# A rotary-embedding kernel bound by its transfers: tables on every fourth partition, and a store issued only when the loads in front of it are nearly done

## The chip, the cores and the metric

The kernel runs on one core of one Trainium2 chip. The metric is the device time of one execution in microseconds (us). The profile's span, first instruction to last, is 1.7 to 2.2 us shorter than the time; what lies between is not in the trace. All runs quoted here are of the fast state, with a granted clock of 1.0.

## The reference, cut to what matters

```python
batch, seq, heads, dim = (16, 512, 16, 64)
x1, x2 = x[..., :32], x[..., 32:]
a, b = x1[..., :16], x1[..., 16:]          # cos, sin: [512, 32], of which the first 16 columns are used
first  = a * cos[..., :16] - b * sin[..., :16]
second = a * sin[..., :16] + b * cos[..., :16]
out = concatenate([first, second, x2])     # x2 passes through
```

`x` has 33.55 MB. It is read once and written once.

## The kernel before

It cuts `x` into T = 4 tiles of 8.39 MB (128 partitions x 64 KB: K = 16 sequence positions of 4 KB each) and turns them in place in a ring of three tile buffers. All loads and stores of `x` go through one queue, that of SyncE (SP), in the order of the program (67.11 MB in the page's q1; store 0, issued at 44.14 us, has its first packet at 51.71, when the first engine has ended the loads in front). The two tables go through the software queue of GpSimd (POOL; 0.13 MB in q0). PB = 32 rows of a table hold 16 positions each; REP = 4 copies of them fill 128 partitions.

```python
stage = const_pool.tile([PB, 2, K, HF], fp32)
table = const_pool.tile([P, 2, K, 2, Q], fp32)
# ...
nc.gpsimd.dma_start(out=stage[:, 0].rearrange("p k j -> p (k j)"), in_=cosf)
nc.gpsimd.dma_start(out=stage[:, 1].rearrange("p k j -> p (k j)"), in_=sinf)
load(0, 0, K0)              # K0 = 4: the first quarter of tile 0
load(0, K0, K)
load(1)
load(2, 0, KC)              # KC = 8: half of tile 2
for r in range(REP):
    nc.vector.tensor_copy(out=table[r * PB : (r + 1) * PB]..., in_=stage...)   # cut
# rotate(t, lo, hi): four VectorE instructions on rows lo..hi of tile t (mul, mul, sub, add)
rotate(0, 0, K0)
rotate(0, K0, (K0 + K) // 2)
rotate(0, (K0 + K) // 2, K)
store(0)
load(2, KC, K)              # stands behind store 0
load(3)                     # takes tile 0's buffer: waits until store 0 has landed
for t in range(1, T):
    rotate(t, 0, KC)
    rotate(t, KC, K)
    store(t)
```

The transfers therefore change direction three times: loads to store 0 at about 52 us, store 0 to loads at about 71 us, loads to store 1 at about 100 us. These three places are called the joints below.

Of the kernel before, what the change touches and what calls it, by code (L numbers as in the profile page):

```python
# [1 line left out]

# [4 lines left out]


@with_exitstack
def kernel(  # L10
    ctx: ExitStack,
    tc: tile.TileContext,
    x: bass.AP,
    cos: bass.AP,
    sin: bass.AP,
    out: bass.AP,
):
    nc = tc.nc
    fp32 = mybir.dt.float32
    P = 128  # L20
    B, S, H, D = x.shape
    Q = D // 4
    HF = D // 2



    K = 16
    T = B * S // (P * K)
    PB = S // K
    REP = P // PB  # L30
    R = H * D
    NS = 3
    KC = K // 2
    K0 = K // 4

    xf = x.rearrange("b s h d -> (b s h d)").rearrange("(t p f) -> t p f", t=T, p=P)
    of = out.rearrange("b s h d -> (b s h d)").rearrange("(t p f) -> t p f", t=T, p=P)
    cosf = cos.rearrange("(p k) j -> p (k j)", k=K)
    sinf = sin.rearrange("(p k) j -> p (k j)", k=K)

    const_pool = ctx.enter_context(tc.tile_pool(name="const", bufs=1))
    b_pool = ctx.enter_context(tc.tile_pool(name="bp", bufs=1, space=bass.MemoryType.PSUM))


    ring = const_pool.tile([P, NS, K, H, D], fp32)
    stage = const_pool.tile([PB, 2, K, HF], fp32)
    table = const_pool.tile([P, 2, K, 2, Q], fp32)

    def rows(t, lo, hi):
        return ring[:, t % NS, lo:hi].rearrange("p k h d -> p (k h d)")  # L50

    def load(t, lo=0, hi=K):
        nc.sync.dma_start(out=rows(t, lo, hi), in_=xf[t, :, lo * R : hi * R])  # L53

    def store(t, lo=0, hi=K):
        nc.sync.dma_start(out=of[t, :, lo * R : hi * R], in_=rows(t, lo, hi))

    nc.gpsimd.dma_start(out=stage[:, 0].rearrange("p k j -> p (k j)"), in_=cosf)  # L58
    nc.gpsimd.dma_start(out=stage[:, 1].rearrange("p k j -> p (k j)"), in_=sinf)  # L59
    load(0, 0, K0)  # L60
    load(0, K0, K)
    load(1)
    load(2, 0, KC)


    for r in range(REP):
        nc.vector.tensor_copy(  # L67
            out=table[r * PB : (r + 1) * PB].rearrange("p t k c j -> p (t k) c j"),
            in_=stage.rearrange("p t k j -> p (t k) j")[:, :, 0:Q]
            .unsqueeze(2)  # L70
            .to_broadcast((PB, 2 * K, 2, Q)),
        )
    C = table[:, 0].rearrange("p k c j -> p k (c j)")
    Sn = table[:, 1].rearrange("p k c j -> p k (c j)")

    def rotate(t, lo, hi):
        n = hi - lo
        x1 = ring[:, t % NS, lo:hi, :, 0:HF]
        c = C[:, lo:hi].unsqueeze(2).to_broadcast((P, n, H, HF))
        s = Sn[:, lo:hi].unsqueeze(2).to_broadcast((P, n, H, HF))  # L80
        b_full = b_pool.tile([P, KC, H, HF], fp32, name="b_t")
        b_t = b_full[:, 0:n]
        nc.vector.tensor_mul(out=b_t, in0=x1, in1=s)  # L83
        nc.vector.tensor_mul(out=x1, in0=x1, in1=c)  # L84
        nc.vector.tensor_sub(  # L85
            out=x1[:, :, :, 0:Q], in0=x1[:, :, :, 0:Q], in1=b_t[:, :, :, Q:HF]
        )
        nc.vector.tensor_add(  # L88
            out=x1[:, :, :, Q:HF], in0=x1[:, :, :, Q:HF], in1=b_t[:, :, :, 0:Q]
        )  # L90

    rotate(0, 0, K0)
    rotate(0, K0, (K0 + K) // 2)
    rotate(0, (K0 + K) // 2, K)
    store(0)
    load(2, KC, K)
    load(3)
    for t in range(1, T):
        rotate(t, 0, KC)
        rotate(t, KC, K)  # L100
        store(t)


# [1 line left out]
_INS = ['x', 'cos', 'sin']  # L105
_OUTS = [((16, 512, 16, 64), 'float32')]


# [23 lines left out]
```

## Time and profile before

| | |
|---|---|
| time, median of 6 runs | 161.91 us (161.74 to 162.52) |
| span of the profiled run | 160.1 us |
| DMA engines busy | 97.8% of the span by the SP queue |
| VectorE busy | 110.0 us, 69% |
| 64 KB packet on one engine, usual | 2.418 us |

The page and the chain are shown and read in the prediction below. One more view is needed for what follows: the rate between joints. A window's rate counts each packet where it starts, and the 16 engines start their 64 KB packets in bunches about 2.4 us apart, so I put the edges of the windows between bunches. Each then holds whole packets. Columns: window, its length, VectorE busy (instructions), GpSimd busy (instructions), granted clock, DMA share, GB/s. The kernel before, for the first half of tile 2, for the rest of tile 2 and most of tile 3, and for the last 16 load packets ahead of store 1:

```profile
41.95:51.70 9.75, 9.68 (x4) 0.00 (x0) 1.00 1.01 430
...
80.70:97.50 16.80, 16.70 (x6) 0.00 (x0) 1.00 1.01 437
97.50:100.05 2.55, 0.40 (x1) 0.00 (x0) 1.00 0.97 411
```

Almost nothing is lost ahead of store 0 (430 GB/s; 0.10 us by the packet records). The last window holds 16 packets of 64 KB in 2.55 us, edges included; at 2.418 us each they could not do better than that by more than 0.13 us.

In the text and tables below, "loss" is worked out from the packet records: the summed durations of the packets of a stretch, less their bytes at 2.418 us for 64 KB, divided by 16 engines. A packet that the edge of the stretch cuts counts by the share of its time that lies inside, and the 4-byte writes that close a transfer (192 in the kernel before, 16 after each of 12 transfers) are left out. Idle time of an engine is no part of this loss and is given apart. Each loss is that of one profiled execution. "The loss from 4 us to tile 0's landing" is the measure of what the tables cost. In kernels that load tile 0 whole, about 0.2 us of it is the slow first 64 KB packet, which runs on past 4 us: counted over the packets that start after 4 us alone, it is 0.73 us in the kernel before.

### The profile page before, as it was taken

The numbers are of one execution on the slowest core, as the hardware profiler recorded it, in microseconds if no ns is written. First come the engines' busy times: TensorE is split into PE (matmuls) and PEld (weight loads), VectorE is DVE, ScalarE is ACT, GpSimd is POOL, SyncE is SP. The second block draws the span as 40 slices with busy tenths as digits, with TensorE's granted clock in tenths as the row PEclk, the third lists the DMA queues.
The fourth block names the chain that finished last, engine by engine and source line by source line (L and its number), as shares of the span: only waits on it lengthen the run. The fifth ranks groups of instructions, "written<-read, shape, count | busy, mean of one in ns | idle before, by whom it ended". The sixth has DMA issues, their size and how long they took to land.

```text
span 160.1 us, 109 instructions
## 1 busy us (share of the span) xinstructions
DVE 110.0 (69%) x40; POOL 1.3 (1%) x6
## 2 busy tenths in 40 slices
DVE  0069709999999999999999994799999900000000
POOL 3000000000000000000000000000000000000000
DMA  6999999699699799899996996996996996996991
GB/s 197 385 504 454 393 459 524 262 524 491 295 401 581 328 524 409 377 393 418 483 540 295 491 524 262 524 524 262 524 524 262 524 524 262 524 491 295 524 459 66
DMA packets 1504, 67.24 MB, mean 420 GB/s; under 512 B 192, under 2 KB 192, under 8 KB 224
## 3 DMA queue, kind: packets, MB, share of 16 engines
q1 hardware_dynamic: 1440, 67.11, 97.8%
q0 software_dynamic: 64, 0.13, 0.2%
HBM read 33.69 MB, written 33.55 MB: 420 GB/s over the span
## 4 chain that ended last, share of the span: by engine, by line
DMA 50%; DVE 28%; DVEq 1%; issue 0%; SPq 0%
DMA ring<-in_x_dram 32%; DMA out_dram<-ring 18%; DVE b_t L83 10%; DVE ring L84 10%; DVE ring L85 5%; DVE ring L88 3%; DVEq L127 1%; SPq L53 0%; DVEq L83 0%
## 5 line engine op out<-in xcount | busy, mean ns | idle before, releaser
L83 DVE TENSOR_TENSOR b_t<-ring,table 128x4096 f32<-128x4096 f32 (+2 forms) x9 | 35.6, 3959 | 8.2 <-DMA ring<-in_x_dram 8.0
L84 DVE TENSOR_TENSOR ring<-ring,table 128x4096 f32<-128x4096 f32 (+2 forms) x9 | 35.6, 3950 | 0.3
L85 DVE TENSOR_TENSOR ring<-ring,b_t 128x2048 f32<-128x2048 f32 (+2 forms) x9 | 18.4, 2049 | 0.3
L88 DVE TENSOR_TENSOR ring<-ring,b_t 128x2048 f32<-128x2048 f32 (+2 forms) x9 | 18.4, 2042 | 0.0
L67 DVE COPY table<-stage 32x1024 f32<-32x1024 f32 x4 | 2.7, 684 | 9.2 <-DMA stage<-in_sin_dram 9.1
L58 POOL DMA_DIRECT2D stage<-in_cos_dram x1 | 0.6, 631 | 0.8 <-PEq L127 0.8
L59 POOL DMA_DIRECT2D stage<-in_sin_dram x1 | 0.5, 498 | 0.0
L116 POOL MEMSET const-bfloat16-1.0<- 128x1 bf16 x1 | 0.1, 102 | 0.0
L116 POOL MEMSET const-float32-0.0<- 128x1 f32 x1 | 0.1, 99 | 0.2 <-issue 0.2
L116 POOL MEMSET const-float32-1.0<- 128x1 f32 x1 | 0.1, 99 | 0.0
L116 POOL MEMSET const-uint8-127<- 128x1 uint8 x1 | 0.1, 99 | 0.0
## 6 DMA issues: line engine op xcount, KB each, us to landing
ring<-in_x_dram SPq DMA_DIRECT2D x2, 4096.0 KB, 43.9
ring<-in_x_dram SPq DMA_DIRECT2D x1, 6144.0 KB, 22.4
ring<-in_x_dram SPq DMA_DIRECT2D x1, 2048.0 KB, 8.5
stage<-in_cos_dram POOLq DMA_DIRECT2D x1, 64.0 KB, 6.0
stage<-in_sin_dram POOLq DMA_DIRECT2D x1, 64.0 KB, 7.2
out_dram<-ring SPq DMA_DIRECT2D x4, 36.4
ring<-in_x_dram SPq DMA_DIRECT2D x2, 35.0
```

The source lines that it names most:

```text
L58: nc.gpsimd.dma_start(out=stage[:, 0].rearrange("p k j -> p (k j)"), in_=cosf)
L59: nc.gpsimd.dma_start(out=stage[:, 1].rearrange("p k j -> p (k j)"), in_=sinf)
L67: nc.vector.tensor_copy(out=table[r * PB : (r + 1) * PB].rearrange("p t k c j -> p (t k) c j"), in_=stage.rearrange("p t k j -> p (t k) j" ...
L83: nc.vector.tensor_mul(out=b_t, in0=x1, in1=s)
L84: nc.vector.tensor_mul(out=x1, in0=x1, in1=c)
L85: nc.vector.tensor_sub(out=x1[:, :, :, 0:Q], in0=x1[:, :, :, 0:Q], in1=b_t[:, :, :, Q:HF])
L88: nc.vector.tensor_add(out=x1[:, :, :, Q:HF], in0=x1[:, :, :, Q:HF], in1=b_t[:, :, :, 0:Q])
L116: nc = _bacc.Bacc("TRN2", target_bir_lowering=False, num_devices=1)
L127: with _tile.TileContext(nc) as tc:
```

## The change

Its intent has two parts. The tables are to be written on partitions 0, 4, ..., 124 in place of 0 to 31, and VectorE then shuffles them together. And a store is not to stand in the queue long before its turn: tile 0 is turned whole, so that store 0 is issued at about 50 us, and store 1 waits until 14/16 of tile 3 has landed.

```diff
-    K0 = K // 4
+    KL = 14
-    stage = const_pool.tile([PB, 2, K, HF], fp32)
+    stage = const_pool.tile([P, 2, K, HF], fp32)
+    spun = const_pool.tile([P, 2 * K, Q], fp32)
+    packed = const_pool.tile([PB, 2 * K, Q], fp32)
-    nc.gpsimd.dma_start(out=stage[:, 0]..., in_=cosf)      # cut; sin likewise
-    load(0, 0, K0)
-    load(0, K0, K)
+    nc.vector.memset(stage[:, :, :, 0:Q], 0.0)
+    spread = stage.rearrange("(j b) t k i -> j b t (k i)", b=REP)
+    nc.gpsimd.dma_start(out=spread[:, 0, 0], in_=cosf)
+    nc.gpsimd.dma_start(out=spread[:, 0, 1], in_=sinf)
+    load(0)
+    PQ = PB // REP
+    nc.vector.stream_shuffle(out=spun[:], in_=stage..., mask=[j % PQ * REP for j in range(PB)])
+    for q in reversed(range(REP)):
+        n = PQ * (q + 1)
+        nc.vector.tensor_copy(out=packed[0:n], in_=spun[q * PB : q * PB + n])
     # the four table copies now read packed
-    rotate(0, 0, K0)
-    rotate(0, K0, (K0 + K) // 2)
-    rotate(0, (K0 + K) // 2, K)
-    store(0)
+    turn(0)                       # rotate both halves, then store
     load(2, KC, K)
-    load(3)
-    for t in range(1, T): ...
+    near = load(3, 0, KL)
+    load(3, KL, K)
+    tc.add_manual_dep(turn(1).ins, near.ins.name, ...)     # store 1 waits for near
+    turn(2)
+    turn(3)
```

More of the change, by code (lines that the diff above doesn't have):

```diff
@@ L52, in load @@
     def load(t, lo=0, hi=K):
-        nc.sync.dma_start(out=rows(t, lo, hi), in_=xf[t, :, lo * R : hi * R])
+        return nc.sync.dma_start(out=rows(t, lo, hi), in_=xf[t, :, lo * R : hi * R])
     def store(t, lo=0, hi=K):
-        nc.sync.dma_start(out=of[t, :, lo * R : hi * R], in_=rows(t, lo, hi))
-    nc.gpsimd.dma_start(out=stage[:, 0].rearrange("p k j -> p (k j)"), in_=cosf)
-    nc.gpsimd.dma_start(out=stage[:, 1].rearrange("p k j -> p (k j)"), in_=sinf)
-    load(0, 0, K0)
-    load(0, K0, K)
+        return nc.sync.dma_start(out=of[t, :, lo * R : hi * R], in_=rows(t, lo, hi))
+    nc.vector.memset(stage[:, :, :, 0:Q], 0.0)
[3 more added lines that the diff above has]
+    load(0)
     load(1)
     load(2, 0, KC)
+    PQ = PB // REP
+    nc.vector.stream_shuffle(
+        out=spun[:],
+        in_=stage.rearrange("p t k j -> p (t k) j")[:, :, 0:Q],
+        mask=[j % PQ * REP for j in range(PB)],
+    )
+    for q in reversed(range(REP)):
+        n = PQ * (q + 1)
+        nc.vector.tensor_copy(out=packed[0:n], in_=spun[q * PB : q * PB + n])
     for r in range(REP):
@@ L68 @@
             out=table[r * PB : (r + 1) * PB].rearrange("p t k c j -> p (t k) c j"),
-            in_=stage.rearrange("p t k j -> p (t k) j")[:, :, 0:Q]
-            .unsqueeze(2)
-            .to_broadcast((PB, 2 * K, 2, Q)),
+            in_=packed.unsqueeze(2).to_broadcast((PB, 2 * K, 2, Q)),
         )
@@ L76, in rotate @@
     def rotate(t, lo, hi):
-        n = hi - lo
         x1 = ring[:, t % NS, lo:hi, :, 0:HF]
-        c = C[:, lo:hi].unsqueeze(2).to_broadcast((P, n, H, HF))
-        s = Sn[:, lo:hi].unsqueeze(2).to_broadcast((P, n, H, HF))
+        c = C[:, lo:hi].unsqueeze(2).to_broadcast((P, hi - lo, H, HF))
+        s = Sn[:, lo:hi].unsqueeze(2).to_broadcast((P, hi - lo, H, HF))
         b_full = b_pool.tile([P, KC, H, HF], fp32, name="b_t")
-        b_t = b_full[:, 0:n]
+        b_t = b_full[:, 0 : hi - lo]
         nc.vector.tensor_mul(out=b_t, in0=x1, in1=s)
@@ L90, in rotate, with turn @@
         )
-    rotate(0, 0, K0)
-    rotate(0, K0, (K0 + K) // 2)
-    rotate(0, (K0 + K) // 2, K)
-    store(0)
-    load(2, KC, K)
-    load(3)
-    for t in range(1, T):
+    def turn(t):
         rotate(t, 0, KC)
         rotate(t, KC, K)
-        store(t)
+        return store(t)
+    turn(0)
+    load(2, KC, K)
+    near = load(3, 0, KL)
+    load(3, KL, K)
+    tc.add_manual_dep(
+        turn(1).ins,
+        near.ins.name,
+        mybir.DependencyInfo(mybir.DependencyClass.Sync, mybir.DependencyReason.DATA),
+        reason="the store follows the loads at the DMA engines",
+    )
+    turn(2)
+    turn(3)
 _INS = ['x', 'cos', 'sin']
```

## The prediction

> **What bounds the kernel now.** I read the page's DMA rows first, then its chain of waits, then the order of instructions in time, and last the records of single DMA packets that the trace keeps. The page says that the 16 DMA engines are the whole story:
>
> ```profile
> span 160.1 us, 109 instructions
> ...
> DVE 110.0 (69%) x40; POOL 1.3 (1%) x6
> ...
> DMA  6999999699699799899996996996996996996991
> ...
> q1 hardware_dynamic: 1440, 67.11, 97.8%
> q0 software_dynamic: 64, 0.13, 0.2%
> ```
>
> VectorE (DVE) is busy 110.0 of 160.1 us, the DMA engines 97.8% of the span. The dips to 6 in the DMA row are not idle time: packets are up to 64 KB long and are booked where they start. I checked that in the packet records: between 3 us and 158 us the 16 engines' packets cover the time without a gap that I can find (the summed durations differ from 16 times the elapsed time by under 0.3 us).
>
> The chain of waits names both engines, but this is how it was followed back and not proof that DVE costs anything:
>
> ```profile
> DMA 50%; DVE 28%; DVEq 1%; issue 0%; SPq 0%
> DMA ring<-in_x_dram 32%; DMA out_dram<-ring 18%; DVE b_t L83 10%; DVE ring L84 10%; DVE ring L85 5%; DVE ring L88 3%; DVEq L127 1%; SPq L53 0%; DVEq L83 0%
> ```
>
> The DVE stretches in it (the first tile's 20 us and the last tile's 27 us) lie beside transfers that were already queued. The order in time shows it for the first store:
>
> ```profile
> 0.74 1.88 SPq L53 DMA_DIRECT2D ring<-in_x_dram  x4
> ...
> 9.13 2.77 DVE L67 COPY table<-stage 32x1024 f32<-32x1024 f32 x4 [9.13 <-DMA stage<-in_sin_dram]
> ...
> 23.66 3.37 DVE L83 TENSOR_TENSOR b_t<-ring,table 128x3072 f32<-128x3072 f32 x1 [4.71 <-DMA ring<-in_x_dram]
> ...
> 44.14 0.35 SPq L56 DMA_DIRECT2D out_dram<-ring  x1
> 44.53 28.14 SPq L53 DMA_DIRECT2D ring<-in_x_dram  x2
> 72.77 0.38 SPq L56 DMA_DIRECT2D out_dram<-ring  x1
> ```
>
> Store 0 is issued at 44.14 us, while the packet records have the loads in front of it running until 51.7 to 52.2 us (each engine ends at its own time). So it waits 8 us in the queue and hides the issue cost. The second store, issued at 72.77 us, stands behind the rest of tile 2 and tile 3, which end at 100.1 to 100.6 us.
>
> The budget, from the packet records: a 64 KB packet takes 2.418 us, so 16 engines move 16 x 65536 / 2.418 us = 433.7 GB/s, and the page's 67.24 MB need 155.0 us. The first packet starts at 1.75 us, the last ends at 158.60, the span ends at 160.1. That is 1.75 head + 156.85 transfers + 1.5 tail. Only 156.85 - 155.0 = 1.8 us of the transfers is loss, and this is where it lies, each as the mean over 16 engines:
> - about 0.6 us in the first packet of each engine (1.21 us on average where 16 KB take 0.604 at the full rate), and about 0.1 us of staggered starts;
> - about 0.65 us from 5.0 to 8.6 us, where the two table transfers pass: the 48 packets of 16 KB that start after 5.3 us take 0.777 us on average and not 0.611;
> - about 0.4 us scattered over everything after 23 us, most of it in the 32 KB packets (1.213 to 1.217 us where half of 2.418 is 1.209) and the seams; the rest is engines that end up to 0.54 us before the last.
>
> [...]The trace before has the tables on 0 to 31 and the slow packets just there[...].
>
> **The change, part by part.**
> *Tables on every fourth partition.* Same bytes (0.13 MB). Of the 0.65 us lost around them, I expect half or a little more to go, since the two table transfers also insert themselves between packets (that part stays): -0.35 us, with 0 to -0.65 possible. This is ahead of everything in the queue, so it shifts the end one for one.
> *The extra DVE work.* A memset of 128x512, which the table transfers now wait for[...], four copies of 32x512 (half of the measured 684 ns each, 1.4 us), and the four table copies as before (2.7 us). The tables arrive later too: [...]packets of 64 KB to queue behind (2.4 us each, one for each table, where it was 0.6). Landing at 12 to 13 us and not 9.1, plus 4.7 us, gives tables at 17 to 18 us. Tile 0 lands at about 23 us. Cost on the path: 0, with some 5 us to spare.
> *Tile 0 loaded and turned whole.* Before, its first quarter was turned from 11.9 to 19.0 us; now DVE starts all of it at about 23.3 us. Two halves at 4.43 + 4.42 + 2.29 + 2.28 + gaps = 13.44 us (57.60 to 71.04 before) end at 50.1 us, so store 0 is issued 6 us later. Packets of 64 KB in place of 16 and 48 KB: 8 x (0.611 - 0.604) and 8 x (1.819 - 1.814) = -0.1 us.
> *Is there a hole at 51 us?* Store 0's first packet should come 1.0 to 1.3 us after its issue (the first loads: issued at 0.74, packets from 1.75 to 2.01), that is at 51.2 to 51.4. The loads end at 51.7 to 52.2 less the 0.4 gained, 51.3 to 51.8. They meet with 0.1 to 0.3 us to spare. If they miss, the start-up of a first packet (0.6 us above) comes on top. I put +0.1 us on this, a mean of mostly 0 and sometimes 0.5.
> *Store 1 waits for 14/16 of tile 3.* The last 2/16 take 19.35/8 = 2.4 us of the engines. Landing to issue takes 0.5 (last packet of tile 0 at 23.1, DVE released at 23.6), issue to packet 1.0 to 1.3, and the engines' own spread is 0.5. So it arrives 0.4 us or more before it is needed: 0. What it could win is at most the scattered loss between 81 and 100 us, which is 0.08 us: 0. Tile 3 in packets of 56 and 8 KB: +0.05 us.
> *Later.* DVE moves 6 us later: tile 1 done at 77, tile 2 at 104, tile 3 at 131 us, while stores 2 and 3 are wanted at about 119 and 138.5. Slack 7 us or more: 0.
> Sum: -0.35 - 0.1 + 0.1 + 0.05 = -0.3, rounded up a little to -0.4 because the author placed both joints on purpose: 161.84 - 0.4 = 161.4 us.
>
> **The rivals.**
> *The tables' loss[...].* It could be the software queue itself[...]. For it: all 16 engines' packets are stretched[...]. Then the spread wins nothing: 161.7 to 161.9.
> *A hole in front of a store.* For it: margins of 0.1 to 0.4 us worked out from one trace. Against: both sides of the joint move together, since DVE starts from the same stream. One hole of 0.6 us: about 162.0; both: 162.5.
> *Queued stores slow the loads in front in a way that one profile hides.* Then the gating would win a per cent or more. Against: loads with a store behind them (44 to 52 us, and 81 to 100 us) lose 0.1 us each. Even a perfect stream from 1.75 us on ends at 1.75 + 155.0 + 1.5 = 158.3, which would be 160.0 us timed; over 2% faster (158.6) needs less than the bytes cost.
> *DVE becomes the bound.* It loses the early quarter tile, but slack at the last store is 7 us. Only tables at 28 us or later would eat that.
>
> **Range and chances.** The floor is the perfect stream, 160.0, of which the first-packet loss is untouched: 160.9 is the best that I think likely. Upward, one missed joint with no gain from the tables is 162.3. Prediction 161.4, 160.9 to 162.2. Faster by over 2% contradicts the byte budget (0.01); slower by over 2% needs a 3.2 us hole, a joint missed by far more than I can construct (0.02).
>
> **What would show it.** Packets of the first tile near the tables hardly longer than their neighbours[...], or still stretched by 0.15 to 0.3 us[...]. Store 0 issued near 50 us with the engines continuously busy across 51 us; store 1 issued near 98 and continuous at 99. DVE waiting for tile 0 and not for the tables at its first product. The last packet at about 158.2 us. I am wrong if the engines show an idle stretch at either joint, or if the rate between joints exceeds 433.7 GB/s.

The sum that gives the time came to -0.3, rounded to -0.4, so 161.4 us. VectorE's work counts as 0 in it: of the 4.7 us there the copies, 1.4 + 2.7 = 4.1, are left, and of the landing at 12 to 13 us 9.13 + 2 x (2.4 - 0.6) = 12.7. That half or more of the 0.65 us would go on other partitions was the estimate; no run had shown it. Nor was it shown that 433.7 GB/s can't be exceeded: none of the 768 packets of 64 KB in the trace before is faster than 2.418 us, and that is all. In "What would show it", packets hardly longer than their neighbours speak for the spread, and stretched ones against it.

## The result, and the profile after

The changed kernel takes 161.70 us in the median of 6 runs (161.49 to 162.10), the kernel before 161.91. The ratio is 0.9984, with a 95% interval of 0.9964 to 1.0004. A ratio here is the mean time of one kernel's fast runs over that of the other's of the same rounds, so it is not quite the ratio of the medians. The predicted 161.4 was 0.3 us low; the interval includes no change at all.

The profiled run of the changed kernel happens to be the slowest of its six, 162.10 us. From its page (the fourth and fifth line are the chain of waits by engine and by line):

```profile
span 160.3 us, 113 instructions
...
DVE 112.4 (70%) x43; POOL 1.4 (1%) x6
...
q1 hardware_dynamic: 1440, 67.11, 97.6%
...
DVE 59%; DMA 14%; issue 7%; DVEq 1%
DVE b_t L96 22%; DVE ring L97 22%; DMA ring<-in_x_dram 14%; DVE ring L101 10%; DVE ring L98 4%; DVEq L148 1%; DVEq L96 0%
```

The chain went from 50% DMA to 59% VectorE, while the DMA engines stayed at 97.6%. That is a lesson in reading a chain: VectorE now runs from 23 to 131 us without a stop, so the walk backwards stays on it, but the bound has not moved. The transfers end at 158.87 us, 28 us after VectorE is done.

The order in time, cut to the places where the prediction had put something (columns: start, duration, engine, line, operation):

```profile
0.91 0.48 DVE L61 MEMSET stage<- 128x512 f32 x1 [0.91 <-PEq L137]
...
15.84 0.01 DVE L73 LOAD_MASK_SELECT spun<-stage  x1 [14.44 <-DMA stage<-in_sin_dram]
15.87 0.72 DVE L73 STREAM_SHUFFLE spun<-stage 128x512 f32<-128x512 f32 x1
16.62 1.77 DVE L80 COPY packed<-spun 32x512 f32<-32x512 f32 x4
18.42 2.78 DVE L83 COPY table<-packed 32x1024 f32<-32x1024 f32 x4
23.05 4.43 DVE L96 TENSOR_TENSOR b_t<-ring,table 128x4096 f32<-128x4096 f32 x1 [1.85 <-DMA ring<-in_x_dram]
...
49.94 0.35 SPq L58 DMA_DIRECT2D out_dram<-ring  x1
...
98.96 31.98 SPq L58 DMA_DIRECT2D out_dram<-ring  x3
```

The tables are ready at 21.2 us, 1.85 us ahead of tile 0. Store 0 is issued at 49.94 us, store 1 at 98.96.

The rates between joints, in windows set as before; the first is tile 1, the others most of tile 3's first load and its last 16 larger packets' worth:

```profile
22.10:42.20 20.10, 19.01 (x6) 0.00 (x0) 1.00 1.00 417
...
81.00:97.90 16.90, 16.76 (x6) 0.00 (x0) 1.00 1.00 434
97.90:100.40 2.50, 2.47 (x2) 0.00 (x0) 1.00 0.97 410
```

The joint at 100 us is as clean as before. Tile 1 at 417 GB/s is not part of the change: it cost this run about 0.8 us, and later kernels with the same program up to that point show 434 there and lose 0.03 us or less (e3, f4). I take it for a disturbance of this one run. In front of it the loss from 4 us to tile 0's landing fell from 0.69 to 0.25 us, and tile 0's last packet landed at 22.58 and not at 23.09. Less the 0.8 us, the last packet would end at about 158.1 us, where 158.2 was predicted. The other five executions, which were timed but not profiled, had spans of 159.7 to 160.1 us. With the same 1.46 us from the last packet to the end, their last packets ended at about 158.2 to 158.6 (an estimate), so they lost 0.1 to 0.5 us in places that no trace shows; see "Open" below.

So far the prediction looks right, and its reason, the tables, too. The experiments show that this is half of the story.

### The profile page after: what moved, and what is told of

Read it like the earlier page. It is cut to its first block, busy times and chain, and to the rows that moved or that the text cites. A ratio compares the mean times of both kernels' runs of the same rounds, so it can differ in the third digit from the quotient of the medians.

```text
span 160.3 us, 113 instructions
## 1 busy us (share of the span) xinstructions
DVE 112.4 (70%) x43; POOL 1.4 (1%) x6
## 3 DMA queue, kind: packets, MB, share of 16 engines
q1 hardware_dynamic: 1440, 67.11, 97.6%
## 4 chain that ended last, share of the span: by engine, by line
DVE 59%; DMA 14%; issue 7%; DVEq 1%
DVE b_t L96 22%; DVE ring L97 22%; DMA ring<-in_x_dram 14%; DVE ring L101 10%; DVE ring L98 4%; DVEq L148 1%; DVEq L96 0%
## 5 line engine op out<-in xcount | busy, mean ns | idle before, releaser
L96 DVE TENSOR_TENSOR b_t<-ring,table 128x4096 f32<-128x4096 f32 x8 | 35.5, 4432 | 2.1 <-DMA ring<-in_x_dram 1.9
L97 DVE TENSOR_TENSOR ring<-ring,table 128x4096 f32<-128x4096 f32 x8 | 35.4, 4424 | 0.3
L98 DVE TENSOR_TENSOR ring<-ring,b_t 128x2048 f32<-128x2048 f32 x8 | 18.3, 2287 | 0.3
L101 DVE TENSOR_TENSOR ring<-ring,b_t 128x2048 f32<-128x2048 f32 x8 | 18.2, 2280 | 0.0
L83 DVE COPY table<-packed 32x1024 f32<-32x1024 f32 x4 | 2.7, 684 | 0.1
L80 DVE COPY packed<-spun 32x512 f32<-32x512 f32 (+3 forms) x4 | 1.7, 416 | 0.1
L61 DVE MEMSET stage<- 128x512 f32 x1 | 0.5, 485 | 0.9 <-PEq L137 0.9
L73 DVE STREAM_SHUFFLE spun<-stage 128x512 f32<-128x512 f32 x1 | 0.7, 723 | 0.0
```

The lines of the kernel that those rows point to most:

```text
L61: nc.vector.memset(stage[:, :, :, 0:Q], 0.0)
L73: nc.vector.stream_shuffle(out=spun[:], in_=stage.rearrange("p t k j -> p (t k) j")[:, :, 0:Q], mask=[j % PQ * REP for j in range(PB)],)
L80: nc.vector.tensor_copy(out=packed[0:n], in_=spun[q * PB : q * PB + n])
L83: nc.vector.tensor_copy(out=table[r * PB : (r + 1) * PB].rearrange("p t k c j -> p (t k) c j"), in_=packed.unsqueeze(2).to_broadcast((PB, ...
L96: nc.vector.tensor_mul(out=b_t, in0=x1, in1=s)
L97: nc.vector.tensor_mul(out=x1, in0=x1, in1=c)
```

## The experiments

All ran with five rounds, results correct throughout, and their ratios are to the kernel before. The first forecast in the expectations of e1, e2, e4 and the x6 runs is that of the spread theory: the loss at the tables depends on the partitions that they are written to. The first four shared a chip, the next four, and the last four.

### e1_tables_only: the kernel before, with the tables spread and nothing else

```diff
 # kernel before, with the new stage, spun, packed, memset, spread, shuffle and copies
 # unchanged: load(0, 0, K0), load(0, K0, K); the three rotates of tile 0; early store 0; no gate
```

> The kernel before with the tables on every fourth partition and nothing else of the change. [...]the 16 KB packets that follow the table packets fall from 0.777 us towards 0.611, the slow-packet loss between 4 and 14 us from 0.69 us to 0.25-0.35, tile 0 lands at about 22.6-22.8 us and not 23.1, time 0.3-0.5 us under the kernel before (ratio 0.997-0.998). Rival (the tile loaded whole, in 64 KB packets, is what helped): the loss stays at 0.6-0.7 us and the ratio is 1.000. Rival (the gated stores helped): 1.000 too, but with the loss near the tables gone.

Measured: 162.61 us, ratio 1.0042 (1.0030 to 1.0054). The first half of the spread theory's forecast held better than expected: the loss from 4 us to tile 0's landing fell from 0.69 to 0.07 us, and tile 0 landed at 22.26 us. And yet the kernel became slower. Tile 1 and the first half of tile 2, windows between bunches:

```profile
22.00:41.30 19.30, 18.84 (x8) 0.00 (x0) 1.00 1.00 435
41.30:52.30 11.00, 10.90 (x5) 0.00 (x0) 1.00 1.00 381
```

The half tile needed 11.00 us, where the kernel before needed 9.75. In the packet records the last two 32 KB packets of every one of the 16 engines are stretched, from 1.213 to between 1.6 and 2.2 us, and then store 0 runs at the full rate. The loss at this joint is 1.30 us (0.10 before). Store 0 was issued at 43.24 us, 9 us before its first packet (52.31), about as early as in the kernel before (7.6 us). None of my theories had expected this.

### e2_no_spread: the changed kernel with the tables back on partitions 0 to 31

```diff
-    nc.vector.memset(...); spread = ...; nc.vector.stream_shuffle(...); the four packed copies
+    nc.gpsimd.dma_start(out=stage[:, 0]..., in_=cosf)      # as before; sin likewise
```

> The changed kernel with the tables back on partitions 0 to 31 (no memset, no shuffle). [...]slow-packet loss between 4 and 14 us back at 0.5-0.7 us, tile 0 landed at about 23.0, ratio to before 1.000 (within 0.001). Rival (packet size or whole tile): loss stays near 0.25 us and the ratio at 0.998.

Measured: 163.25 us, ratio 1.0085 (1.0072 to 1.0098). The loss before tile 0's landing is back at 0.70 us and tile 0 lands at 23.12, as the spread theory has it. The rest of the cost was not expected: 0.90 us is lost at the joint at 71 us, from store 0 to the loads. Some engines fall behind there: the rest of tile 2 ends at 81.3 us on the first and 83.0 on the last engine, and the stores end 0.98 us apart (0.54 before). This also opened a hole at the joint at 100 us. Store 1 waits for the slowest engine's part of the gated load, which ended at 99.95 us, 1.7 us after the fastest engine's (0.4 us in the changed kernel). So it was issued late:

```profile
100.39 4.30 SPq L56 DMA_DIRECT2D out_dram<-ring  x2
```

The loads of the faster engines ran out from 100.76 us on, and the first packet of the store started at 101.23. In between as few as 5 of the 16 engines had a packet, 0.22 us of idle time in the mean of the 16. The hole that the prediction had feared did not open in the changed kernel, but it did here.

### e3_no_gate: the changed kernel without the gate on store 1

```diff
-    near = load(3, 0, KL)
-    load(3, KL, K)
-    tc.add_manual_dep(turn(1).ins, near.ins.name, ...)
+    load(3)
+    turn(1)
```

> The changed kernel without the gate on store 1: tile 3 in one load, store 1 issued as soon as DVE is done, at about 77 us, 20 us ahead of its turn. My theory: no difference to the changed kernel beyond 0.1 us (ratio to before 0.998), loads from 84 to 100 us at 432-434 GB/s with the store queued behind them. Rival (queued stores slow the loads in front of them): these loads under 430 GB/s and the time at least 0.3 us above the changed kernel.

Measured: 163.01 us, ratio 1.0074 (1.0061 to 1.0087), 1.3 us over the changed kernel's median. My theory fell: the gate that I had booked at zero is what keeps the changed kernel from being slower than before. The store's issues (first line), and the loads of tile 3 but for the last 16 packets, and those packets:

```profile
76.76 54.12 SPq L58 DMA_DIRECT2D out_dram<-ring  x3
```

```profile
80.50:97.40 16.90, 16.76 (x6) 0.00 (x0) 1.00 1.00 434
97.40:100.70 3.30, 3.27 (x2) 0.00 (x0) 1.00 1.05 318
```

Store 1 is issued at 76.76 us, and the loads run at 434 GB/s for 17 us with the store behind them. Only the last packet of each engine suffers: the 16 packets take 3.30 us, not 2.50. In the records they last 3.0 to 3.8 us and not 2.42, a loss of 1.04 us. The rival was right that queued stores cost the loads in front, but not all of these loads: only the last 64 KB of each engine, next to the store.

### e4_even_ports: the tables on every second partition of 0 to 63

```diff
-    spread = stage.rearrange("(j b) t k i -> j b t (k i)", b=REP)
+    spread = stage.rearrange("(j b) t k i -> j b t (k i)", b=2)     # and [0:PB] of it
-    PQ = PB // REP
+    PQ = PB // 2
-    for q in reversed(range(REP)):
+    for q in reversed(range(2)):
```

> The changed kernel with the tables on every second partition of 0 to 63 (still a correct result). [...]like e2, loss between 4 and 14 us 0.5-0.7 us, ratio 1.000. Rival (what matters is that neighbouring partitions are not written together, or the write being strided): like the changed kernel, loss 0.25 us, ratio 0.998.

Measured: 163.44 us, ratio 1.0100 (1.0078 to 1.0121). The loss before tile 0's landing is 0.71 us (e2: 0.70), though the ratio of 1.000 that I expected was missed as in e2. So it is neither a distance of two between the partitions that helps nor the memset and the shuffle, which this run has too: what counts is which partitions are written (every fourth of 128 lost 0.25 us in the changed kernel). The joint at 71 us loses 1.01 us, and the joint at 100 us has a hole of 0.38 us in the mean, both again as in e2. The profiled execution is the slowest of the six (164.17 us).

### x6_packed, x6_spread, x6_even: six more table loads

```diff
+    room = ring.rearrange("(j b) n k h d -> j b n (k h d)", b=1)    # spread: b=4; even: b=2
+    for n in range(6):                      # into the half of tile 2's buffer that is loaded later
+        at = (2 * KC + n) * K * HF
+        more = nc.gpsimd.dma_start(out=room[0:PB, 0, 2, at : at + K * HF], in_=sinf)
+        # more waits for the memset, so that it comes after the real tables
```

> The changed kernel, plus six more loads of the sine table through the software queue, onto partitions 0 to 31 of a part of the ring that is overwritten later (result stays right). Bytes alone: 6 x 64 KB at 433.7 GB/s = 0.91 us. [...] (the kernel before lost about 0.3 us for each table beyond its bytes: +2.7 us). Rival (the cost is that of the software queue, wherever it writes): the same as x6_spread.

> The same six loads onto every fourth partition. [...]0.15 us for each transfer: +0.9 to +1.3 us over the changed kernel, 0.9-1.5 us under x6_packed. Rival (software queue): no difference to x6_packed.

> The same six loads onto every second partition of 0 to 63[...]. [...]as x6_packed within 0.3 us. Rival (spacing of the partitions is what counts): as x6_spread.

Tile 1, beside which most of the six transfers run, in x6_packed, x6_spread and x6_even:

```profile
22.50:44.00 21.50, 19.91 (x6) 0.00 (x0) 1.00 1.01 405
```

```profile
22.40:42.35 19.95, 18.71 (x6) 0.00 (x0) 1.00 1.01 436
```

```profile
22.50:43.80 21.30, 19.64 (x6) 0.00 (x0) 1.00 1.01 408
```

From 15.4 to 45 us the loss beyond the bytes is 1.76 us packed, 1.56 us even and 0.06 us spread, so 0.29, 0.26 and 0.01 us for each transfer of 64 KB. Through the same software queue, on spread partitions, a table cost no more here than its bytes. So the rival of the software queue is out, and so is a spacing of two. Why the first two sets cost something and the third does not is not shown: both lie below partition 64 and the third reaches to 124, but it also has a step of four, and a set that would part the two was not tried.

The times do not show it: ratios 1.0152 (1.0132 to 1.0172), 1.0138 (1.0118 to 1.0158) and 1.0152 (1.0134 to 1.0170). x6_spread was 1.4 us ahead at 44 us and lost 1.00 us at the joint at 71 us, where the other two lost 0.06; its engines then ended 0.97 us apart. I had expected it 0.9 to 1.5 us under x6_packed.

### e5_gate_full: store 1 behind the whole of tile 3

```diff
-    near = load(3, 0, KL)
-    load(3, KL, K)
+    near = load(3)
```

> The changed kernel with store 1 issued only when all of tile 3 has landed, not 14/16 of it. My theory of the joint: landing to issue 0.5 us, issue to first packet 1.0-1.3 us, so a hole of 1.3-1.6 us at about 101 us and up to 0.6 us more in the first packets: 1.3-2.2 us over the changed kernel, and the issue times of the changed kernel had 0.4-0.9 us to spare. Rival (the queue is deep enough, or DVE sets the end, so that the hole is made up later): no difference.

Measured: 166.32 us, ratio 1.0274 (1.0260 to 1.0288). This did not test what I meant. The scheduler put store 2 ahead of store 1 in the queue, and store 2 waits for VectorE to finish tile 2:

```profile
103.66 0.82 SPq L58 DMA_DIRECT2D out_dram<-ring  x2
```

The order of the two is taken from the times of issue. All engines stood idle from 100.27 us, when tile 3 had landed, to 104.50; in the mean of the 16 it was 4.5 us. What it does show: a hole at a joint goes to the end in full (idle 4.5 us, time 4.7 us over the changed kernel by the ratios), and from issue to first packet on an empty queue take 0.84 to 0.99 us. With the 0.54 us from landing (98.42) to issue (98.96) in the changed kernel, store 1's packets can start at 99.8 to 99.95 us there, and the loads end at 100.45 to 100.90. The gate has 0.5 us or more to spare there; e2 and e4, whose engines were further apart, had less than none.

### f1_tables_gate0 and f2_tables_both_gates: e1 with one gate, with both

```diff
 # f1: e1, and
-    load(2, 0, KC)
+    near0 = load(2, 0, KC - 2)
+    load(2, KC - 2, KC)
-    store(0)
+    hold(store(0), near0)                  # the same manual dependency
 # f2: also
-    load(3)
+    near = load(3, 0, 14)
+    load(3, 14, K)
     # and hold(store(1), near)
```

> e1 (tables spread, else the kernel before) with store 0 held until 6/8 of the first half of tile 2 has landed. e1 lost 1.3 us in the last loads in front of store 0, which was queued 8 us ahead. New theory (a store queued well ahead slows the last loads in front of it when the 16 engines run nearly in step): the loss at 52 us falls under 0.2 us, but the engines then come to the joint at 100 us still in step and lose about 1.0 us there, as e3 did, so the time stays near e1: 162.2-163.0. Rival (the loss at 52 us has another cause, such as the tile cut at a quarter): 1.3 us lost at 52 us as in e1.

> f1 with store 1 held too, until 14/16 of tile 3 has landed, as in the changed kernel. New theory: neither load-to-store joint loses over 0.2 us, the time is 161.2-161.7, the changed kernel's or a little under it. Rival: 162.4 or more, as e1.

f1 measured 162.03 us, ratio 1.0010 (0.9998 to 1.0022), just below what I expected: the loss at 52 us fell from 1.30 to 0.09, and at 100 us, where nothing is held, it rose to 0.50. f2 measured 161.38 us (161.35 to 161.44), ratio 0.9969 (0.9956 to 0.9982). It is the only version here that is clearly faster than the kernel before, by 0.3%; that it beats the changed kernel (0.9984, in other rounds) is not shown: their intervals overlap, and they were not measured side by side. Its load joints, at 52 us and at 100:

```profile
41.30:51.10 9.80, 9.73 (x4) 0.00 (x0) 1.00 1.00 426
...
80.25:97.15 16.90, 16.75 (x6) 0.00 (x0) 1.00 1.00 434
97.15:99.65 2.50, 1.45 (x1) 0.00 (x0) 1.00 0.97 406
```

No joint stands out: 9.80 us for the half tile where e1 took 11.00.

### f3_before_both_gates: the kernel before, with both stores held

```diff
 # kernel before (tables on partitions 0 to 31), with f2's near0, near and hold
```

> The kernel before, tables on partitions 0 to 31, with both stores held. The kernel before lost under 0.1 us at its joints though both stores were queued far ahead; its engines are about 0.5 us apart there. New theory: nothing to win at the load-to-store joints, ratio to before 0.999-1.002, unless the store-to-load joint at 71 us loses as in e2 (+0.9 us, 162.8). Rival (gating is worth a per cent by itself): 160.5-161.2.

Measured: 162.94 us, ratio 1.0062 (1.0049 to 1.0075). The joints at 52 and 100 us lose 0.12 and 0.05 us, as they did without gates. There was nothing to win, and the joint at 71 us, which I had named as the exception, loses 0.64 us in place of 0.07. The loss at the tables is 0.82 us, that of packed tables. So gating is worth nothing by itself; it pays where the store would have cost something.

### f4_gate_early: the gate at 8/16 in place of 14/16

```diff
-    KL = 14
+    KL = 8
```

> The changed kernel with store 1 held only until 8/16 of tile 3 has landed, so that it is queued some 8 us before its turn and not under 1 us (20 us in e3 without a gate). New theory (being queued before the last packets of the loads start is enough): the last loads lose about 1.0 us, time 162.6-163.4 as e3. Rival (only a long stay in the queue costs, or the gate helps through the split of the load): as the changed kernel, 161.5-161.9.

Measured: 162.69 us, ratio 1.0047 (1.0035 to 1.0059). The issue of store 1, then tile 3 but for its last two rounds of packets, and those:

```profile
91.28 39.75 SPq L58 DMA_DIRECT2D out_dram<-ring  x3
```

```profile
80.60:97.50 16.90, 16.76 (x6) 0.00 (x0) 1.00 1.01 434
97.50:101.05 3.55, 3.52 (x2) 0.00 (x0) 1.00 1.04 295
```

A gate that lets the store into the queue 9.8 us before its first packet (101.09) loses as much as none: 1.29 us at this joint. The gate's use is in its lateness and not in cutting the load as such. This cut leaves packets of 32 KB, where the one at 14/16 leaves packets of 8 KB, so the small packets are a rival that f4 alone does not rule out. The joint at 52 us does: in the changed kernel, e2, e3, e4 and f4 the half of tile 2 is not cut, its last packets have 32 KB, store 0 is late, and 0.02 to 0.12 us is lost, where e1 with the same packets and an early store loses 1.30.

### The joints together

Loss in us in the 5 us on either side of each joint, in the profiled run. "Early" means that the store was in the queue over 7 us before its first packet, "late" 3 us or less. These are single executions: those of e2 (163.55) and e4 (164.17 us) were among the slowest of their kernels, that of e3 (162.70) the fastest of its five. The x6 runs and e5 are left out.

| kernel | tables, 4 us to tile 0 landed | joint at 52 | joint at 71 | joint at 100 | ratio to before |
|---|---|---|---|---|---|
| before | 0.69 | 0.10 early | 0.07 | 0.06 early | 1 |
| changed | 0.25 | 0.12 late | 0.02 | 0.06 late | 0.9984 |
| e1 | 0.07 | 1.30 early | 0.02 | 0.06 early | 1.0042 |
| e2 | 0.70 | 0.05 late | 0.90 | 0.11 late, and 0.22 idle | 1.0085 |
| e3 | 0.24 | 0.07 late | 0.38 | 1.04 early | 1.0074 |
| e4 | 0.71 | 0.05 late | 1.01 | 0.10 late, and 0.38 idle | 1.0100 |
| f1 | 0.09 | 0.09 late | 0.22 | 0.50 early | 1.0010 |
| f2 | 0.08 | 0.09 late | 0.21 | 0.09 late | 0.9969 |
| f3 | 0.82 | 0.12 late | 0.64 | 0.05 late | 1.0062 |
| f4 | 0.24 | 0.02 late | 0.60 | 1.29 early | 1.0047 |

Four of the seven early stores cost 0.5 to 1.3 us; at none of the thirteen late ones are the loads stretched by more than 0.12. In these runs, standing early in the queue was thus needed for the loss, and not enough. Lateness has its own price where the engines are far apart: the holes of e2 and e4.

## Why the prediction was right, and where its steps were not

**The bound** was right. The transfers fill the span in every run but e5 and, for the 0.2 to 0.4 us at one joint, e2 and e4.

**The tables** were right in direction and too small in size. The prediction gave -0.35 us, since it held that half of the loss came from the table packets' standing between the others (in the trace before, 4 KB packets that start from 5.34 to 5.91 us and from 6.93 to 7.48, with 16 KB packets on either side) and would stay. Nearly nothing stayed: 0.07 of 0.69 us in e1, whose packets are those of the kernel before, and 0.06 of 0.73 in the changed kernel by the packets that start after 4 us. Tile 0 landed 0.51 us earlier. The x6 runs show that it is not the software queue (0.01 us for each spread table beyond its bytes). Which property of the partitions it is, they do not show.

**The VectorE work** was off the path, as predicted, but the term for the tables' landing was mis-sized: 12 to 13 us predicted (9.13 + 2 x (2.4 - 0.6) gives 12.7; the memset took 0.48), 15.84 measured, and tables ready at 21.2 and not at 17 to 18. The packet records show why. I had counted one 64 KB packet of waiting for each table, but a table's data and its closing write each take a turn of their own behind one: cosine data at 7.3 us, its close at 9.9, sine data at 12.3, its close from 14.9 to 15.3. The slack was 1.85 us in place of the 5 promised.

**Store 0** was right: 50.1 us predicted, 49.94 measured, no hole. The disturbance in tile 1 gave this joint 0.8 us that it would not have had, but e3, with the same program up to there and no such disturbance, shows no hole either (store issued at 49.87, its first packet at 51.07, all 16 engines busy).

**The gate on store 1** is the step that failed, in the words "What it could win is at most the scattered loss between 81 and 100 us, which is 0.08 us: 0". I read that from the kernel before, where an early store happens to cost nothing. In the changed kernel without the gate, and with tile 3 in one load, the same store costs 1.0 us at its joint and 1.3 us in time (e3). The rival that I had set aside, queued stores that slow the loads in front, was right about this kernel, except that a profile does not hide it: the last packets of the loads show it, once it occurs.

**The sum** held in part by luck. A gate worth 0 is right only against the kernel before, whose early stores cost nothing for a reason that I do not know; the loads ahead of the changed kernel's two stores are clean because the stores are late. And the prediction has no term at all for the joint at 71 us. An estimate from the traces: tile 0 landed 0.51 us earlier, and if the joint at 71 us costs the changed kernel what it costs e3, 0.38 us where the kernel before loses 0.07, then 0.20 us are left. The medians are 0.21 us apart, where 0.4 was predicted. Either half of the change alone loses: e1 has the better tables and 0.7 us more time, e2 has the late stores and 1.4 us more.

**Open.** Why three early stores cost nothing (both of the kernel before, and store 1 in e1) was not found. While planning the last runs I held that engines running nearly in step make the loss. It fits six of the seven: the last 64 KB of the loads start 0.30, 0.37 and 0.40 us apart over the 16 engines where 1.30, 1.04 and 0.50 us are lost, and 0.45, 0.51 and 0.53 apart where nothing is. But in f4 they start 0.48 us apart and 1.29 us are lost, so it does not separate the cases.

The joint at 71 us, where loads stand behind a store, is open too. It loses between 0.02 and 1.01 us without a gate of any kind, its loads having been queued 20 us or more in every kernel. Holding the load there until store 0 is nearly done would have been the next experiment. The changed kernel's 0.02 there comes from the disturbed run; e3, e5 and f4, with the same program up to 72 us, show 0.38, 0.44 and 0.60. With e3's figure in place of the disturbance the profiled execution would have taken 162.10 - 0.80 + 0.36 = 161.66 us (an estimate), next to the median of 161.70. There is a pattern that no run was made to test: in the two kernels whose store 0 is early (before, e1) this joint loses 0.07 us or less, and in nine of the twelve whose store 0 is late it loses 0.21 to 1.01. The other three (changed, x6_packed, x6_even) are the ones that had just lost 0.8 to 1.8 us in and around tile 1. So a late store 0 may be paid for one joint later.

Last, the time exceeds the span by 1.75 us in some profiled runs (e2) and by 2.2 in others (e3); I have no reason for it, and the losses at the joints are read from the packets and not from the times.

## What to carry to other kernels

Here the queue of transfers was the bound (97.8 and 97.6% of the span), and VectorE had time to spare: 2.4 us more of its work (110.0 to 112.4) did not show in the time (161.91 and 161.70 us). But the moment at which a transfer entered the queue counted: a store queued over 7 us ahead of its first packet went with a loss of 0.5 to 1.3 us in the last loads in front of it in four of seven cases, and holding it until 1.5 to 2.1 us before its first packet avoided that here. The gate waited for the slowest engine, and where the engines were far apart (1.7 us in e2) it left the others idle (0.2 and 0.4 us in e2 and e4). A clean joint in one trace is no proof that the joint is safe: a gain of 0.6 us at the tables in e1 came with a loss of 1.3 at a joint that had been clean. So test such a change in its parts, and look at the last packets ahead of every change of direction.
